# First attention of a two-layer backbone: the source's order of instructions is kept on every engine there too

## The chip, the cores and the metric

The kernel runs on one core of a Trainium2 chip. Its time is the device time of one execution in microseconds. Three runs of the kernel before took 1642.66, 1642.76 and 1645.69 us; the median is 1642.76 us. The profile was taken in an execution of its own, which took 1646.84 us.

## What is computed

The reference runs two layers over 1024 latent tokens and 256 context tokens of width 1024. Layer 0 is a windowed attention with grouped heads (16 query heads, 4 key/value heads of width 64) and a sink logit for each head; layer 1 is a latent attention. The change lies in the attention of layer 0, which for each block of 128 queries is this, cut to what matters:

```python
def attend_block(args):
    q, k, v, m = args                      # k, v: previous, own and next block of 128 keys
    s_loc = jnp.einsum("bqhgd,bkhd->bhgqk", q, k) * scale
    s_loc = jnp.where(m, s_loc, -jnp.inf)
    s_ctx = jnp.einsum("bqhgd,bchd->bhgqc", q, kc) * scale
    p = softmax_with_sink(jnp.concatenate([s_loc, s_ctx], axis=-1), sink_b)
    return (jnp.einsum("bhgqk,bkhd->bqhgd", p[..., :3 * BLOCK], v)
            + jnp.einsum("bhgqc,bchd->bqhgd", p[..., 3 * BLOCK:], vc))
...
yx = (ox * jax.nn.silu(gx)) @ w_out
```

Context queries attend to the 256 context keys alone. The result of the layer, `x + gate * yx`, goes into layer 1.

## The kernel before

**Stages.** The kernel builds normalized inputs, projects them to queries, keys, values and gates (loop over `order`, lines 772 to 797), runs the first attention with its output projection (loop over `units`, from line 816), projects for layer 1, runs the second attention and ends with the output projection of layer 1. Products are made in two or three pieces: every operand is split into a high part (a cast, ScalarE, line 121) and a remainder (a subtraction, VectorE or GpSimd, line 122), and `mm3` multiplies high by high, low by high and high by low (lines 126 to 128).

**The first attention.** There are ten tiles of 128 tokens (two of context, eight of latents), taken in the order 2, 0, 3, 1, 4, 5, 6, 7, 8, 9, and four groups of heads for each: 40 units, `UnitA`. A unit covers four heads. A latent tile inside the sequence has five chunks of 128 keys (three local, two context); tiles 2 and 9, at the ends, have four; a context tile has two. In what follows units are counted from 0 in this order, so units 0 to 3 are tile 2, units 4 to 7 context, 8 to 11 tile 3, 12 to 15 context, 16 to 35 the five inner tiles 4 to 8, 36 to 39 tile 9.

A unit goes through these steps, each with its engine:

- `score(h)`, four times: two matmuls each (591, 592) for the 256 context keys and for the local keys, two VectorE operations (598) that mask, move the scores to SBUF and keep a running minimum, and one ScalarE exponential (599). Three PSUM banks (0, 1, 2) take the scores in turn.
- `T(ci)` for each chunk: four TensorE transposes (618), a ScalarE cast (121) and a VectorE subtraction (122).
- `PV(ci)` for each chunk: two matmuls (628) that add into the one bank that `psv` has, bank 5.
- `post` and `post2`: a GpSimd subtraction (605), a small ScalarE exponential for the sink (606), a GpSimd addition (610), a VectorE reciprocal (611) and a GpSimd copy (613).
- `fin`: four ScalarE copies (638, 639 twice) that take the result out of bank 5.
- `fin2`, in the next unit: two transposes (647), a ScalarE copy (649) and five GpSimd operations (651, 652, 653, 655, 656).

The output projection of a tile is a generator (`outproj`), of which a part is taken between the steps of the next tile's units: groups of six matmuls (126 to 128), and at each half's end a VectorE product (676) and a GpSimd addition (677).

The source is software pipelined. While unit `u` does its transposes and products, it also issues scores 2 and 3 of the next unit `nu` (lines 830 to 832) and scores 0 and 1 of the one after, `nnu` (850 to 853); transposes run two chunks ahead (`next_T`). Within an inner unit with five chunks the source says, chunk by chunk: score 2 of `nu`, `fin2` of the unit before, T, PV(0), `post`; score 3 of `nu`, T, PV(1), `post2`; T, PV(2), score 0 of `nnu`; T, PV(3); T, PV(4), score 1 of `nnu`; `fin`.

**What sets the order.** The kernel is written in Tile. Tile finds the dependencies and sets the semaphores, and its scheduler orders the instructions of each engine by its own estimate of when they are ready, so that what stands in an engine's stream need not stand there in the order of the source. Inside `tc.manual_schedule()` every engine's instructions keep the order in which the source issues them. Before the change this holds from line 770 to line 801: for the first projection, and for the four scores of unit 0 that are written there. All later code, the first attention included, is ordered by the scheduler. On the chip each engine then takes its stream as it stands.

The function that holds all of this, with its line numbers, is this:

Of the kernel before, what the change touches and what calls it, by code (L numbers as in the profile page):

```python
# [33 lines left out]
class Ring:  # L34
# [6 lines left out]
    def next(self):  # L41
        b = self.bufs[self.i % len(self.bufs)]
        self.i += 1
        return b


def shp(ap, *dims):
    n = 1
    for d in dims:
        n *= d  # L50
    ap = ap[:, 0:n]
    if len(dims) == 1:
        return ap
    names = "abcdefg"[: len(dims)]
    kw = {c: d for c, d in zip(names[1:], dims[1:])}
    return ap.rearrange("p (" + " ".join(names) + ") -> p " + " ".join(names), **kw)
# [3 lines left out]
def kernel(ctx: ExitStack, tc: tile.TileContext, t, out, dbg=None):  # L60
# [63 lines left out]
    def mm3(o, a, b, first, last):  # L124
        (ah, al), (bh, bl) = a, b
        nc.tensor.matmul(o, ah, bh, start=first, stop=False)  # L126
        nc.tensor.matmul(o, al, bh, start=False, stop=False)  # L127
        nc.tensor.matmul(o, ah, bl, start=False, stop=last)  # L128
# [132 lines left out]
    def src0(i):  # L261
        if i < 2:
            return t["ctx"][i * 128 : i * 128 + 128, :]
        return t["x"][(i - 2) * 128 : (i - 1) * 128, :]
# [12 lines left out]
    def next_item():  # L277
        item[0] += 1
        todo = [x for x in due if x[0] <= item[0]]
        due[:] = [x for x in due if x[0] > item[0]]  # L280
        for _, fn in todo:
            fn()
# [375 lines left out]
    def outproj(ti, og, last=False):  # L658
        x = xr0.next()
        load(out=x, in_=src0(ti))  # L660
        gate = gx if ti >= 2 else gc
        cs = [slice(c * 512, c * 512 + 512) for c in range(2)]
        order = [(0, 0, 8), (1, 0, 8)]
        if last:
            order = [(0, 0, 6), (1, 0, 6), (0, 6, 8), (1, 6, 8)]
        ps = [None, None]
        for c, ka, kb in order:
            if ka == 0:
                ps[c] = PB[:, 0, :] if last and c else pso()
            for k in range(ka, kb):  # L670
                mm3(ps[c], [og[:, s, k, :] for s in range(2)], [Wo[k][:, s, cs[c]] for s in range(2)], k == 0, k == 7)
                if k % 2:
                    yield
            if kb == 8:
                y = ytmp.next()
                nc.vector.tensor_mul(y, ps[c], gate[:, cs[c]])
                (nc.vector if last else nc.gpsimd).tensor_add(x[:, cs[c]], x[:, cs[c]], y)
        load(out=x1_d[ti * 128 : ti * 128 + 128, :], in_=x)
# [91 lines left out]
    in_order = tc.manual_schedule()  # L770
# [27 lines left out]

    while due:
        next_item()  # L800
    in_order.__exit__(None, None, None)
    units[1].score(0)
    units[1].score(1)
    tq = iter([(u, c) for u in units for c in range(u.m)])
# [1 line left out]
    def next_T():  # L806
        n = next(tq, None)
        if n:
            n[0].T(n[1])
# [6 lines left out]
    for ui, u in enumerate(units):  # L816
        if ui in (1, 2):
            next(wo_fill, None)
            next(wo_fill, None)
        if u.g == 0:  # L820
            og = shp(ogr.next(), 2, 8, 128)
            steps = 4 * u.m - 2
            done = 0
        nu = units[ui + 1] if ui + 1 < len(units) else None
        nnu = units[ui + 2] if ui + 2 < len(units) else None
        at = {}
        for h in range(2, 4):
            at.setdefault(min(h - 2, max(0, u.m - 3)), []).append(h)
        for ci in range(u.m):
            if nu:  # L830
                for h in at.get(ci, ()):
                    nu.score(h)
            if ci == 0:
                while fins:
                    fins.pop()()
                if nnu:
                    nnu.prep()
                if ui + 3 < len(units):
                    units[ui + 3].prep_q()
            i = u.g * u.m + ci - 1  # L840
            if u.m == 2 and i > 0 and done < -(-8 * i // steps):
                next(filler, None)
                done += 1
            next_T()
            u.PV(ci)
            if ci == 0:
                u.post()
            if ci == 1:
                u.post2()
            if nnu:  # L850
                for h, at0 in enumerate((max(0, u.m - 3), u.m - 1)):
                    if ci == at0:
                        nnu.score(h)
            while i > 0 and done < -(-8 * i // steps):
                next(filler, None)
                done += 1
        u.fin(og)
        fins.append(u.fin2)
        if u.g == 3:
            for _ in filler:  # L860
                pass
            filler = outproj(u.ti, og, last=nu is None)
    units[-1].fin2(fast=True)
    last_outproj = filler

# [694 lines left out]
```

## Time and profile before

| | us |
|---|---|
| median of three runs | 1642.76 |
| the profiled execution | 1646.84 |
| its span, first to last instruction | 1645.1 |
| TensorE matmuls busy | 1587.5 (96%) |
| VectorE busy | 948.7 (58%) |
| ScalarE busy | 825.1 (50%) |
| GpSimd busy | 829.5 (50%) |
| from the end of the first projection to the last transposes (647) of the first attention | 366.92 to 731.27 in the span |

The profile names the engines PE (TensorE matmuls), PEld (its weight loads), DVE (VectorE), ACT (ScalarE), POOL (GpSimd) and SP (the queue that issues most DMAs). `L598` is line 598. A row of the timeline gives the start in us from the start of the span, how long the row lasts, the engine, the line, the operation, what is written and read, the shape, and in brackets how long the engine had been idle and what ended that. Rows of the same operation that follow one another are merged, with their count behind an x. An operation can start before the one ahead of it on its engine has quite ended, so the time from start to start is the cost of one. A unit's place in the trace is found by the pair of transposes L647: the first of them, at 378.97 us, stands in unit 1, the last, at 731.27 us, behind unit 39.

### The profile page before, as it was taken

What the parts mean: (1) busy time and instruction counts of PE and PEld (TensorE: products, weight loads), DVE (VectorE), ACT (ScalarE), POOL (GpSimd) and SP (SyncE); (2) the same over time, 40 slices, a digit from 0 to 9 for tenths busy, and PEclk for the clock granted to TensorE, in tenths of its full rate; (3) what the DMA queues carried; (4) which work ended last, traced back from release to release, by engine and by line L of the source; (5) the groups of instructions that cost most, each with busy time, mean ns of one, the idle gap of its engine ahead of it and who ended that gap; (6) DMA issues with size and microseconds to landing.
All of it is one profiled execution on the core that took longest, in us unless ns stands there. A gap on an engine that the chain in (4) does not pass through costs nothing.

```text
span 1645.1 us, 23587 instructions
## 1 busy us (share of the span) xinstructions
PE 1587.5 (96%) x8156; PEld 1214.1 (74%) x8156; DVE 948.7 (58%) x1692; ACT 825.1 (50%) x1779; POOL 829.5 (50%) x896
## 2 busy tenths in 40 slices
PE   7899999988999999998999999999999999999998
PEld 2687888776878888878887887566766756666687
DVE  1786778537757777768444005655455455455354
ACT  3622122239877778777323324555555555555421
POOL 1453356214654444444245422786676777668510
PEclk9999999989999999999999999999999999999999
DMA  8535544364333333235127722211111111122151
GB/s 280 169 115 181 170 163 167 126 197 140 94 116 95 96 91 91 90 112 173 52 78 249 233 66 87 77 52 36 39 39 36 45 37 39 46 80 70 47 160 64
DMA packets 122464, 176.74 MB, mean 107 GB/s; under 512 B 11484, under 2 KB 71516, under 8 KB 122344
## 3 DMA queue, kind: packets, MB, share of 16 engines
q1 hardware_dynamic: 120184, 171.12, 32.5%
q10 hardware_dynamic: 2160, 4.11, 0.8%
q8 instruction: 64, 1.05, 0.3%
q14 instruction: 56, 0.46, 0.1%
HBM read 129.04 MB, written 46.15 MB: 106 GB/s over the span
## 4 chain that ended last, share of the span: by engine, by line
PE 78%; DVE 6%; ACT 6%; issue 4%; POOL 3%; DMA 2%; POOLq 0%; DVEq 0%; SPq 0%; ACTq 0%
PE PB L126 17%; PE PB L128 16%; PE PB L127 16%; PE PB L1233 9%; PE PB L628 4%; PE PB L1199 4%; PE PB L618 3%; PE PB L591 2%; PE PB L592 2%; ACT arena_r L121 1%; DVE arena_r L122 1%; ACT arena_f L599 1%; DVE arena_f L202 1%; DVE arena_f L385 1%; PE PB L1258 1%
## 5 line engine op out<-in xcount | busy, mean ns | idle before, releaser
L126 PE MATMUL PB<-arena_r 128*128 128x512 f32 (+3 forms) x1632 | 607.3, 373 | 7.2 <-ACT arena_r L205 3.8
L127 PE MATMUL PB<-arena_r 128*128 128x512 f32 (+3 forms) x1632 | 597.2, 366 | 4.5 <-DVE arena_r L207 3.1
L128 PE MATMUL PB<-arena_r 128*128 128x512 f32 (+3 forms) x1632 | 594.7, 366 | 0.2 <-DVE arena_r L122 0.2
L126 PEld LDWEIGHTS PB<-arena_r 128*128 128x128 f32 (+1 forms) x1632 | 310.1, 190 | 98.3 <-issue 32.8
L1225 POOL TENSOR_TENSOR arena_f<-arena_f 128x512 f32<-128x512 f32 x252 | 327.1, 1298 | 75.2 <-ACT arena_f L1218 60.1
L128 PEld LDWEIGHTS PB<-arena_r 128*128 128x128 f32 (+1 forms) x1632 | 309.5, 190 | 49.8 <-issue 0.9
L127 PEld LDWEIGHTS PB<-arena_r 128*128 128x128 f32 (+1 forms) x1632 | 310.8, 190 | 47.0 <-DVE arena_r L207 4.5
L1218 ACT ACTIVATE arena_f<-PB 128x512 f32<-128x512 f32 x320 | 188.9, 597 | 125.2 <-PE PB L128 112.9
L1203 DVE TENSOR_REDUCE arena_f<-PB 128x1 f32<-128x1280 f32 x128 | 190.5, 1488 | 104.2 <-PE PB L1199 101.7
L122 DVE TENSOR_TENSOR arena_r<-PB,arena_r 128x512 fp32r<-128x512 f32 (+4 forms) x255 | 163.4, 647 | 138.0 <-ACT arena_r L121 136.5
L122 POOL TENSOR_TENSOR arena_r<-arena_f,arena_r 128x512 fp32r<-128x512 f32 x84 | 116.6, 1400 | 184.1 <-ACT arena_r L121 164.9
L121 ACT CAST arena_r<-PB 128x512 fp32r<-128x512 f32 (+4 forms) x255 | 139.5, 551 | 73.6 <-PE PB L618 36.9
L598 DVE CUSTOM_DVE_ANT_0 arena_f<-PB,arena_f,small 128x256 f32<-128x256 f32 (+1 forms) x288 | 145.1, 524 | 30.8 <-PE PB L592 23.0
L1233 PE MATMUL PB<-arena_f 128*64 128x512 f32 x640 | 157.1, 600 | 0.0
L599 ACT ACTIVATE arena_f<-arena_f,small 128x640 f32<-128x640 f32 (+2 forms) x160 | 119.1, 747 | 27.0 <-DVE small L598 26.6
L628 PE MATMUL PB<-arena_r 128*128 128x512 f32 x336 | 122.7, 439 | 5.6 <-ACT arena_f L639 5.3
L385 DVE SCALAR_TENSOR_TENSOR arena_f<-arena_f,small 128x512 f32<-128x512 f32 x98 | 114.1, 1209 | 11.3 <-DMA arena_f<-ada_w 11.0
L121 ACT CAST arena_r<-arena_f 128x512 fp32r<-128x512 f32 (+1 forms) x124 | 72.8, 608 | 75.0 <-DMA arena_f<-a_w_in 21.1
L618 PE MATMUL PB<-ident,arena_f 128*128 128x128 f32 x672 | 107.2, 275 | 1.2 <-ACT arena_f L649 0.6
L1233 PEld LDWEIGHTS PB<-arena_f 128*64 128x64 f32 x640 | 43.5, 136 | 80.9 <-issue 79.4
L1199 PE MATMUL PB<-arena_r 96*128 96x512 f32 (+1 forms) x384 | 99.8, 367 | 0.3 <-DVE arena_f L1203 0.2
L618 PEld LDWEIGHTS PB<-ident,arena_f 128*128 128x128 f32 x672 | 83.2, 141 | 18.2 <-ACT arena_f L599 2.3
(150 smaller groups left out, 1751.7 us busy)
## 6 DMA issues: line engine op xcount, KB each, us to landing
arena_r<-q_d SPq DMA_DIRECT2D x160, 128.0 KB, 2.9
arena_f<-ada_w SPq DMA_DIRECT2D x68, 256.0 KB, 3.0
arena_f<-a_w_in SPq DMA_DIRECT2D x40, 256.0 KB, 3.7
arena_f<-x SPq DMA_DIRECT2D x16, 512.0 KB, 4.6
q_d<-arena_f SPq DMA_DIRECT2D x16, 512.0 KB, 2.6
qn_d<-arena_f SPq DMA_DIRECT2D x16, 512.0 KB, 5.0
arena_r<-qn_d SPq DMA_DIRECT2D x32, 256.0 KB, 3.6
arena_f<-ada_w SPq DMA_DIRECT2D x14, 512.0 KB, 6.2
```

The costliest lines, as they stand in the source:

```text
L121: nc.scalar.copy(hi, src)
L122: (lo_eng or nc.vector).tensor_sub(lo, src, hi.bitcast(F32))
L126: nc.tensor.matmul(o, ah, bh, start=first, stop=False)
L127: nc.tensor.matmul(o, al, bh, start=False, stop=False)
L128: nc.tensor.matmul(o, ah, bl, start=False, stop=last)
L618: nc.tensor.transpose(pt[:, h, :], self.Ps[h][:, ci * 128 : ci * 128 + 128], ident)
L628: nc.tensor.matmul(self.pv, V[:, self.chunks[ci], self.g, :], PT[:, s], start=ci == 0 and s == 0, stop=ci == self.m - 1 and s == 1,)
L1199: nc.tensor.matmul(psm[:, n0 : n0 + n], self.qT[0:96, 0, b * 128 : b * 128 + 128], kt[0:96, 0, n0 : n0 + n], start=True, stop=True,)
L1203: nc.vector.reduce_max(self.mx[:, 96 + b : 97 + b], psm[:, 0:TOK], AX.X, negate=True)
L1218: nc.scalar.activation(E, S, AF.Exp)
L1225: eng.tensor_add(self.acc, self.acc, E)
L1233: nc.tensor.matmul(self.pv[p : p + 64], Vq[:, c, self.h % 4, :], self.E.pop(c), start=c < 2, stop=c >= NT - 2)
```

## The change

The end of the part in which the source's order is kept moves from line 801, ahead of the first attention, to a place behind the loop over its units. The last unit's `fin2` and what follows are ordered by the scheduler as before. No instruction is added, removed or altered.

```diff
     while due:
         next_item()
-    in_order.__exit__(None, None, None)
     units[1].score(0)
     units[1].score(1)
     tq = iter([(u, c) for u in units for c in range(u.m)])
...
             for _ in filler:
                 pass
             filler = outproj(u.ti, og, last=nu is None)
+    in_order.__exit__(None, None, None)
     units[-1].fin2(fast=True)
     last_outproj = filler
```

Two places show what the streams look like. The first is ScalarE's at the border between two units of an inner tile (`fin` is 638 and 639, the exponentials of the scores are 599, the cast of a transpose 121, the copy of `fin2` 649, the sink's exponential 606). Before:

```order
L121 CAST arena_r<-PB 128x512
L638 COPY arena_f<-PB 64x256
L639 COPY arena_f<-PB 64x256
L638 COPY arena_f<-PB 64x256
L639 COPY arena_f<-PB 64x256
L649 COPY arena_f<-PB 128x256
L121 CAST arena_r<-PB 128x512
L599 ACTIVATE arena_f,small<-arena_f,small 128x640 x2
L121 CAST arena_r<-PB 128x512
L599 ACTIVATE arena_f,small<-arena_f,small 128x640
L606 ACTIVATE small<-small 128x4
```

And after the change, at the same border:

```order
L599 ACTIVATE arena_f,small<-arena_f,small 128x640
L638 COPY arena_f<-PB 64x256
L639 COPY arena_f<-PB 64x256
L638 COPY arena_f<-PB 64x256
L639 COPY arena_f<-PB 64x256
L599 ACTIVATE arena_f,small<-arena_f,small 128x640
L649 COPY arena_f<-PB 128x256
L121 CAST arena_r<-PB 128x512
L606 ACTIVATE small<-small 128x4
L599 ACTIVATE arena_f,small<-arena_f,small 128x640
L121 CAST arena_r<-PB 128x512 x2
```

The exponential of `nnu`'s score 1 has moved ahead of the four copies of `fin`, that of `nu`'s score 2 ahead of 649, and 606 has moved from behind the exponential of score 3 to a place ahead of it.

The second place is TensorE's stream at the same border (591 and 592 are the score matmuls, 628 the products with V, 647 the transposes of `fin2`, 618 those of a chunk). Before:

```order
L628 MATMUL PB<-arena_r 128x512 x2
L591 MATMUL PB<-arena_r 128x256
L592 MATMUL PB<-arena_r 128x256
L591 MATMUL PB<-arena_r 128x384
L592 MATMUL PB<-arena_r 128x384
L591 MATMUL PB<-arena_r 128x256
L592 MATMUL PB<-arena_r 128x256
L647 MATMUL PB<-ident,arena_f 128x128 x2
L618 MATMUL PB<-ident,arena_f 128x128 x4
L591 MATMUL PB<-arena_r 128x384
L592 MATMUL PB<-arena_r 128x384
L628 MATMUL PB<-arena_r 128x512 x2
```

And after:

```order
L628 MATMUL PB<-arena_r 128x512 x2
L591 MATMUL PB<-arena_r 128x256
L592 MATMUL PB<-arena_r 128x256
L591 MATMUL PB<-arena_r 128x384
L592 MATMUL PB<-arena_r 128x384
L591 MATMUL PB<-arena_r 128x256
L592 MATMUL PB<-arena_r 128x256
L591 MATMUL PB<-arena_r 128x384
L592 MATMUL PB<-arena_r 128x384
L647 MATMUL PB<-ident,arena_f 128x128 x2
L618 MATMUL PB<-ident,arena_f 128x128 x4
L628 MATMUL PB<-arena_r 128x512 x2
```

The fourth pair of score matmuls has moved from behind the transposes to a place ahead of them; the rest is the same.

GpSimd's stream for a unit is alike in both: 651, 652, 653, 655, 656 of the unit before, then 605, 610 and 613 of this one.

## The prediction

> **What bounds the kernel now.** I read the page first, then the busy time of each stage of the first attention, then the timeline of one border between two units.
>
> ```profile
> span 1645.1 us, 23587 instructions
> PE 1587.5 (96%) x8156; PEld 1214.1 (74%) x8156; DVE 948.7 (58%) x1692; ACT 825.1 (50%) x1779; POOL 829.5 (50%) x896
> ```
>
> TensorE is busy 96% of the span. The stretches below run from the last matmul of the first projection to the first L647, then unit by unit as the front counts them: units 1 to 3, 4 to 7 (context), 8 to 11, 12 to 15 (context), 16 to 35, 36 to 39. Columns are length, then busy time and count of PE, PEld, DVE, ACT and POOL, then the granted clock and the DMA's share and rate.
>
> ```profile
> 366.92:378.97 12.05, 10.57 (x61) 8.45 (x60) 8.81 (x27) 10.56 (x21) 1.49 (x2) 0.86 0.52 153
> 378.97:403.28 24.31, 20.95 (x128) 16.45 (x127) 18.47 (x61) 22.30 (x61) 14.79 (x27) 1.00 0.42 125
> 403.28:429.37 26.09, 23.52 (x136) 19.33 (x137) 15.93 (x53) 22.20 (x66) 17.83 (x36) 1.00 0.32 91
> 429.37:468.31 38.94, 38.39 (x233) 33.06 (x232) 28.41 (x81) 30.74 (x77) 19.77 (x35) 1.00 0.31 96
> 468.31:496.67 28.36, 26.77 (x149) 21.42 (x147) 16.27 (x57) 20.72 (x62) 17.11 (x33) 1.00 0.43 131
> 496.67:699.51 202.84, 200.14 (x1202) 173.99 (x1201) 155.01 (x451) 161.85 (x384) 95.96 (x171) 1.00 0.31 92
> 699.51:731.27 31.76, 31.11 (x184) 26.10 (x183) 20.50 (x64) 23.26 (x59) 16.83 (x30) 1.00 0.19 65
> ```
>
> Units 16 to 35 take 202.84 / 20 = 10.14 us each, and TensorE is idle for 2.7 us of the 202.84: they are bound by TensorE, with ScalarE 80% and VectorE 76% busy beside it. So nothing is to be won there, and the question is whether the source's order still lets ScalarE, VectorE and GpSimd run ahead of TensorE. The front stages leave TensorE idle for 1.48 + 3.36 + 2.57 + 0.55 + 1.59 = 9.6 us.
>
> The border between two inner units, on TensorE (transposes of the last chunk's turn, product with V, transposes of `fin2`, next transposes, PV(0) of the new unit):
>
> ```profile
> 556.56 0.60 PE L618 MATMUL PB<-ident,arena_f 128*128 128x128 f32 x4
> 556.91 0.71 PE L628 MATMUL PB<-arena_r 128*128 128x512 f32 x2
> 557.47 0.28 PE L591 MATMUL PB<-arena_r 128*128 128x256 f32 x1
> ...
> 558.06 0.28 PE L591 MATMUL PB<-arena_r 128*128 128x256 f32 x1
> ...
> 558.31 0.38 PE L647 MATMUL PB<-ident,arena_f 128*128 128x128 f32 x2
> 558.52 0.60 PE L618 MATMUL PB<-ident,arena_f 128*128 128x128 f32 x4
> ...
> 559.47 0.68 PE L628 MATMUL PB<-arena_r 128*128 128x512 f32 x2
> ```
>
> and on ScalarE:
>
> ```profile
> 557.25 0.59 ACT L121 CAST arena_r<-PB 128x512 fp32r<-128x512 f32 x1 [0.35 <-PE PB L618]
> 557.86 0.37 ACT L638 COPY arena_f<-PB 64x256 f32<-64x256 f32 x1
> ...
> 559.00 0.37 ACT L639 COPY arena_f<-PB 64x256 f32<-64x256 f32 x1
> 559.39 0.37 ACT L649 COPY arena_f<-PB 128x256 f32<-128x256 f32 x1
> ...
> 560.13 0.84 ACT L599 ACTIVATE arena_f<-arena_f,small 128x640 f32<-128x640 f32 x1
> ...
> 560.96 0.83 ACT L599 ACTIVATE arena_f<-arena_f,small 128x640 f32<-128x640 f32 x1
> ...
> 561.77 0.58 ACT L121 CAST arena_r<-PB 128x512 fp32r<-128x512 f32 x1
> 562.25 0.83 ACT L599 ACTIVATE arena_f<-arena_f,small 128x640 f32<-128x640 f32 x1
> ...
> 563.17 0.21 ACT L606 ACTIVATE small<-small 128x4 f32<-128x4 f32 x1
> ```
>
> ScalarE empties bank 5 (638, 639) at once, until 559.37, and PV(0) of the next unit, which writes that bank, starts 0.10 us later. 606 comes last, behind three exponentials.
>
> **The change, step by step.** No instruction goes or comes; each engine takes its stream in another order. In the new order ScalarE's stream, from one 606 to the next, is: 606, exponential of score 3, casts, exponential of `nnu`'s score 0, two casts, exponential of `nnu`'s score 1, `fin`, exponential of `nu`'s score 2, 649, a cast, 606. Two waits close this into a loop. First, `fin` stands behind an exponential that waits for two VectorE operations, which wait for the subtraction of the last transposes. Second, 606 waits for 605, which stands on GpSimd behind the five operations of `fin2`, which wait for `fin` and for 649; and behind 606 on ScalarE are queued the exponential of score 3 and the casts that the next transposes and products need. The VectorE and GpSimd prices:
>
> ```profile
> 554.70 0.47 DVE L598 CUSTOM_DVE_ANT_0 arena_f<-PB,arena_f,small 128x256 f32<-128x256 f32 x1
> ...
> 555.32 0.62 DVE L598 CUSTOM_DVE_ANT_0 arena_f<-PB,arena_f,small 128x384 f32<-128x384 f32 x1
> ...
> 557.87 0.69 DVE L122 TENSOR_TENSOR arena_r<-PB,arena_r 128x512 fp32r<-128x512 f32 x1 [0.42 <-ACT arena_r L121]
> 558.48 0.47 DVE L598 CUSTOM_DVE_ANT_0 arena_f<-PB,arena_f,small 128x256 f32<-128x256 f32 x1
> ...
> 563.69 0.18 DVE L611 RECIPROCAL small<-small 128x4 f32<-128x4 f32 x1 [0.61 <-POOL small L610]
> ```
>
> ```profile
> 555.98 0.83 ACT L599 ACTIVATE arena_f<-arena_f,small 128x640 f32<-128x640 f32 x1 [0.49 <-DVE small L598]
> ```
>
> ```profile
> 560.14 0.74 POOL L652 TENSOR_TENSOR arena_f<-arena_f 128x256 f32<-128x256 f32 x1
> ...
> 562.93 0.21 POOL L605 TENSOR_TENSOR small<-small 128x4 f32<-128x4 f32 x1
> ```
>
> A score's two VectorE operations, one behind the other, and on to the exponential: (555.32 - 554.70) + (555.98 - 555.32) = 1.28. Cast to its subtraction: 557.87 - 557.25 = 0.62; subtraction to the next: 0.61. Exponential to the next: 0.82 (560.13, 560.96, 561.77). `fin`: 557.86 to 559.37, 1.51. GpSimd from 652 to 605: 2.79; 605 to 606: 562.93 to 563.17, 0.24.
>
> The loop of a full inner unit is then: 606 0.21; exponential 0.82; cast to subtraction 0.62; two subtractions 1.22; the reciprocal between them 0.18; score 0 of `nnu` 1.28; its exponential 0.82; casts and subtractions of two transposes 0.62 + 1.22; score 1 of `nnu` 1.28; its exponential 0.82; `fin` 1.51; exponential 0.82; 649 0.37; GpSimd 2.79; and 0.24. Sum 14.82 us, against 10.14 now. TensorE stays ahead of this loop: its own work in a unit is the 10.0 us of the present (200.14 / 20), and it waits mainly at PV(0), for `fin`. The loop decides, and 20 units cost 20 x 4.68 = **93.6 us** more.
>
> The other stages, by the same loop with the terms that their units have. Exponentials of shorter rows cost (mean in ns behind the bar's first number):
>
> ```profile
> L599 ACT ACTIVATE arena_f<-arena_f,small 128x512 f32<-128x512 f32 x24 | 17.4, 725 | 4.4 <-DVE small L598 4.3
> L599 ACT ACTIVATE arena_f<-arena_f,small 128x256 f32<-128x256 f32 x32 | 16.2, 508 | 1.2 <-DVE small L598 1.1
> ```
>
> - Units 1 to 3 (four chunks): one subtraction less (0.61), four exponentials of 512 (0.4 less) and two shorter VectorE operations (0.2 less): 13.6. Where `nnu`, then `nu` too, is a context unit, a second VectorE operation and longer exponentials fall away: 12.0 and 11.5. With four casts of weights (0.62 each) that stand in the stream, 39.6 against 24.31: **+15.3**.
> - Context units: 0.21 + 0.50 + 0.62 + 0.61 + 0.57 (one VectorE operation of 0.47 and the 0.10 of a hand-off, as from 559.37 to 559.47) + 0.50 + 1.51 + 1.0 + 0.37 + 2.79 + 0.24 = 8.9; 10.3 and 10.9 for the last two, which score full units. Four take 39.0, against 26.09 and 28.36: **+12.9** and **+10.6**.
> - Units 8 to 11: 14.8, 14.8, 12.7, 12.1 (the last two score context): 54.5 against 38.94, **+15.5**.
> - Units 36 to 39: 13.6 twice, then no more scores of `nnu`; 10 for unit 38 and 7 for the last, which have few or no exponentials to wait for (estimates on both sides of the present 31.76 / 4 = 7.9): 44.2 against 31.76, **+12.4**.
> - Ahead of the first L647 there is no `fin2` yet; the scores and casts of unit 1 stand in line. Between 0 and 3 us more; I take **+1.5**.
> - Behind the attention the code is scheduled as before, and its loads go into buffers that the last exponentials free: between -3 and +3, taken as **0**.
>
> SP's queue keeps the source's order too, with `prep_q` three units and `prep` two units ahead, that is over 20 us, for transfers that land within 2.9 us of their issue (the last column):
>
> ```profile
> arena_r<-q_d SPq DMA_DIRECT2D x160, 128.0 KB, 2.9
> ```
>
> I cost it at nothing. If a store of `x1_d` that waits for GpSimd held loads up, that cover would be gone; it is in the upper end. The two VectorE products of `outproj` a tile, one of which falls into the loop, are in the upper end as well (0.6 us a tile, 5 us in all).
>
> Sum: 93.6 + 15.3 + 12.9 + 10.6 + 15.5 + 12.4 + 1.5 = 161.8 us. The profiled execution took 1646.84 and would take 1808.6; it lies 4.1 us above the median, so I predict 1642.76 + 161.8 = 1804.6, **1805 us**. The own range of this case is 1775 to 1835: 0.1 us more or less at each of some ten hand-offs of the loop would be 1 us in each of 39 units, and I take three quarters of that on either side.
>
> [...]
>
> ```profile
> 353.03:356.44 3.41, 1.22 (x8) 0.84 (x7) 1.43 (x2) 2.90 (x4) 1.27 (x1) 1.00 0.71 194
> 356.44:359.85 3.41, 3.04 (x12) 2.80 (x13) 2.98 (x14) 1.97 (x5) 0.00 (x0) 0.50 0.81 224
> 359.85:363.27 3.42, 3.42 (x18) 3.42 (x17) 0.70 (x5) 1.38 (x5) 0.80 (x3) 0.50 0.98 279
> ```
>
> 2.2 us idle were followed by 6.8 us at half clock. In the new order TensorE idles about 3 us at each border, so this is to be expected there. A half-speed window takes 1.7 us of TensorE's work, and TensorE has about 4.8 us a unit to spare, so the sum stays; a pair of windows is a rival below. [...]
>
> **The rivals.**
>
> *Only the first wait binds.* If GpSimd reaches 605 early enough that 606 holds nothing, a border costs what `fin` waits: from the last transposes 557.25 - 556.56 = 0.69, then 0.62 + 0.61 + 1.28 + 0.82 + 1.51 + 0.10 = 5.63 us, against 2.65 us of TensorE's work ahead of PV(0) (0.35 + 0.56 + 0.21 + 0.35 by the starts above, and two scores of 558.06 - 557.47 = 0.59 each). 2.98 us idle at three borders of four, 1.4 less where a group of output matmuls stands between: 2.6 us on 9.9, 12.5 a unit, +48 for units 16 to 35 and at the same half of the sum +34 elsewhere: **1725 us**. For it: the present trace has 605 in the same place without harm. Against: there 606 stands behind three exponentials. 10%.
>
> *The clock binds as well.* With pairs of half-speed windows TensorE is late by some 2 us in the two units of four that have a group of output matmuls between PV(0) and the last transposes: 20 units, +40, **1845 us**. 9%.
>
> *The source's order is better.* If the loop's parts overlap by 4.7 us a unit or more, so that it is shorter than TensorE's 10.1, only the idle time of the front stages is at stake, 9.6 + 2.7 + 0.6 = 12.9 us at most: **1630 us**. For it: in the middle tiles the two orders are nearly alike. Against: it takes an exponential that doesn't wait for its scores. 3%. That it changes nothing, 2%.
>
> **How the numbers follow.** My forecast has 76%. The low end, 1740, is the own range's end and then half way to the first rival, the high end, 1850, takes in the clock's; left out are the first rival, the better order and no change, 15%, and some of the tails. Differences under 0.2% (3.3 us, about what a measurement of this kernel can tell from none) have 2%, faster 3%, slower 95%.
>
> **What would show it.** In the profile after, a pair of L647 every 14.8 us in units 16 to 35; ScalarE idle ahead of 606 with POOL L605 as what ended it, and ahead of 599 with DVE L598; TensorE idle ahead of 628 with ACT L639; PE busy about 70% of that stretch. Wrong would be: borders every 12.5 us with no idle time ahead of 606 (first rival), or TensorE without idle time at half clock (second), or every 10 us (third).

## The result, and the profile after

The changed kernel took 1867.31 us (median of four runs, 1866.13 to 1869.23) against 1643.76 us before in the same comparison: a ratio of 1.1359, 95% interval 1.1341 to 1.1377. The direction was as predicted, and so was the time of an ordinary unit; the whole lies 62 us above the forecast and above the range's end of 1850. The page of the profile after, its span and the busy time of each engine:

```profile
span 1865.6 us, 23612 instructions
PE 1671.2 (90%) x8156; PEld 1271.3 (68%) x8156; DVE 950.4 (51%) x1692; ACT 829.7 (44%) x1779; POOL 832.4 (45%) x896
```

VectorE, ScalarE and GpSimd are as long busy as before; the span has grown by 220.5 us. The stages, in the same stretches and columns as in the prediction (ahead of the first L647, units 1 to 3, 4 to 7, 8 to 11, 12 to 15, 16 to 35, 36 to 39):

```profile
366.60:387.02 20.42, 11.33 (x62) 9.59 (x61) 10.72 (x32) 11.23 (x22) 2.47 (x4) 0.88 0.29 84
387.02:430.54 43.52, 28.57 (x116) 22.65 (x115) 17.94 (x51) 22.54 (x58) 15.58 (x26) 0.66 0.18 52
430.54:473.97 43.43, 33.14 (x150) 26.29 (x149) 17.20 (x59) 23.01 (x64) 17.62 (x33) 0.84 0.25 73
473.97:535.30 61.33, 45.79 (x229) 38.32 (x228) 27.04 (x78) 30.93 (x76) 18.89 (x34) 0.86 0.20 61
535.30:578.52 43.22, 32.38 (x151) 25.85 (x149) 17.87 (x60) 23.08 (x64) 18.91 (x34) 0.88 0.29 86
578.52:904.41 325.89, 247.96 (x1202) 206.69 (x1200) 155.09 (x451) 161.22 (x380) 94.60 (x170) 0.84 0.19 58
904.41:953.80 49.39, 38.98 (x194) 30.86 (x192) 20.72 (x63) 23.83 (x61) 18.94 (x34) 0.93 0.17 56
```

Every stage of the first attention is longer, and TensorE is idle for 325.89 - 247.96 = 77.9 us in units 16 to 35 where it was idle for 2.7. Behind the last L647 the program takes 1865.6 - 953.80 = 911.8 us, against 913.8. So all of the loss is in the attention. What TensorE and ScalarE wait for in units 16 to 35 (the waits of each engine: total, times, longest):

```profile
ACT arena_f L599 <- DVE small L598: 81.3, 40, 2.4
ACT small L606 <- POOL small L605: 52.1, 20, 2.6
ACT arena_r L121 <- PE PB L618: 29.3, 9, 5.3
```

```profile
PE PB L628 <- ACT arena_f L639: 38.6, 20, 2.3
PE PB L591 <- DVE small L598: 20.1, 19, 2.5
PE PB L126 <- DVE arena_f L676: 19.3, 5, 5.1
```

The first two rows of ScalarE and the first of TensorE are the waits of the forecast loop, 20 times each for 606 and for PV(0). An ordinary unit, on ScalarE, GpSimd and TensorE, from one L647 to the next:

```profile
644.35 0.38 PE L647 MATMUL PB<-ident,arena_f 128*128 128x128 f32 x2
644.64 0.83 ACT L599 ACTIVATE arena_f<-arena_f,small 128x640 f32<-128x640 f32 x1 [2.04 <-DVE small L598]
...
647.13 1.22 PE L628 MATMUL PB<-arena_r 128*128 128x512 f32 x2 [1.96 <-ACT arena_f L639]
...
651.28 0.21 POOL L605 TENSOR_TENSOR small<-small 128x4 f32<-128x4 f32 x1
651.52 0.21 ACT L606 ACTIVATE small<-small 128x4 f32<-128x4 f32 x1 [2.61 <-POOL small L605]
...
655.60 0.83 ACT L599 ACTIVATE arena_f<-arena_f,small 128x640 f32<-128x640 f32 x1 [2.10 <-DVE small L598]
...
659.22 0.38 PE L647 MATMUL PB<-ident,arena_f 128*128 128x128 f32 x2
```

14.87 us from L647 to L647; the forecast loop was 14.82. The forecast did not name TensorE's second row either, the wait of a score's matmul for its bank; ordinary units keep 14.87 us with it. What lengthens units is the last row of each list of waits: L126 waits five times, 19.3 us in all, for VectorE's L676, and casts on ScalarE wait up to 5.3 us for transposes. The five waits of L126 and the five longest of the casts stand in the third unit of each tile (18, 22, 26, 30, 34), which takes 20 to 21 us. Unit 18, between 606 and the late cast:

```profile
615.55 0.21 ACT L606 ACTIVATE small<-small 128x4 f32<-128x4 f32 x1 [2.60 <-POOL small L605]
...
617.07 0.69 DVE L122 TENSOR_TENSOR arena_r<-PB,arena_r 128x512 fp32r<-128x512 f32 x1 [2.22 <-ACT arena_r L121]
617.67 0.17 DVE L611 RECIPROCAL small<-small 128x4 f32<-128x4 f32 x1
617.76 0.66 DVE L676 TENSOR_TENSOR arena_f<-PB,arena_f 128x512 f32<-128x512 f32 x1
...
618.47 0.80 PE L126 MATMUL PB<-arena_r 128*128 128x512 f32 x1 [3.63 <-DVE arena_f L676]
...
619.92 0.63 PE L126 MATMUL PB<-arena_r 128*128 128x512 f32 x1
...
622.35 0.59 ACT L121 CAST arena_r<-PB 128x512 fp32r<-128x512 f32 x1 [5.32 <-PE PB L618]
```

The products of the output projection have one PSUM bank. L676 empties it of a tile's first half; in the source it is issued by the generator step that also begins the second half, and in VectorE's stream it stands behind a subtraction that hangs on 606. So L126 of the second half holds TensorE for 3.63 us, and the transposes queued behind it come late to the loop.

Ahead of the first L647, the timeline shows ScalarE's cast of output weights, VectorE's subtraction of it, and the first scores of unit 1:

```profile
368.65 1.13 ACT L121 CAST arena_r<-arena_f 128x512 fp32r<-128x512 f32 x2
...
369.81 1.34 DVE L122 TENSOR_TENSOR arena_r<-arena_f,arena_r 128x512 fp32r<-128x512 f32 x1 [8.63 <-ACT arena_r L121]
371.07 0.47 DVE L598 CUSTOM_DVE_ANT_0 arena_f<-PB,arena_f,small 128x256 f32<-128x256 f32 x1
...
371.61 0.39 PE L591 MATMUL PB<-arena_r 128*128 128x256 f32 x1 [4.11 <-DVE small L598]
```

VectorE stands idle for 8.63 us at a subtraction of weights while scores wait behind it, and TensorE stops for 4.11 us. In the kernel before, VectorE was idle there for 5.40 us and took scores next, at 367.36 us.

### The profile page after: what moved, and what is told of

It reads as the page before. It is cut to its first block, busy times and chain, and to the rows that moved or that the text cites. A ratio compares the mean times of both kernels' runs of the same rounds, so it can differ in the third digit from the quotient of the medians.

```text
span 1865.6 us, 23612 instructions
## 1 busy us (share of the span) xinstructions
PE 1671.2 (90%) x8156; PEld 1271.3 (68%) x8156; DVE 950.4 (51%) x1692; ACT 829.7 (44%) x1779; POOL 832.4 (45%) x896
## 3 DMA queue, kind: packets, MB, share of 16 engines
q10 hardware_dynamic: 2160, 4.11, 0.7%
## 4 chain that ended last, share of the span: by engine, by line
PE 63%; ACT 12%; DVE 11%; POOL 6%; issue 6%; DMA 2%; SPq 0%; DVEq 0%; ACTq 0%; POOLq 0%
PE PB L126 15%; PE PB L128 14%; PE PB L127 14%; PE PB L1233 8%; ACT arena_f L599 5%; DVE arena_r L122 4%; PE PB L1199 4%; DVE arena_f L598 3%; ACT arena_r L121 2%; PE PB L628 2%; PE PB L618 2%; ACT arena_f L639 1%; POOL arena_f L652 1%; POOL arena_f L653 1%; POOL arena_r L656 1%
## 5 line engine op out<-in xcount | busy, mean ns | idle before, releaser
L126 PE MATMUL PB<-arena_r 128*128 128x512 f32 (+3 forms) x1632 | 612.0, 377 | 38.9 <-DVE arena_f L676 30.2
L126 PEld LDWEIGHTS PB<-arena_r 128*128 128x128 f32 (+1 forms) x1632 | 312.9, 192 | 134.9 <-DVE arena_f L676 34.7
L127 PEld LDWEIGHTS PB<-arena_r 128*128 128x128 f32 (+1 forms) x1632 | 314.0, 192 | 50.3 <-DVE arena_r L207 6.3
L128 PEld LDWEIGHTS PB<-arena_r 128*128 128x128 f32 (+1 forms) x1632 | 312.9, 192 | 51.9 <-issue 1.7
L628 PE MATMUL PB<-arena_r 128*128 128x512 f32 x336 | 143.5, 514 | 56.0 <-ACT arena_f L639 55.7
L121 ACT CAST arena_r<-PB 128x512 fp32r<-128x512 f32 (+4 forms) x255 | 135.2, 547 | 82.9 <-PE PB L618 47.4
L618 PE MATMUL PB<-ident,arena_f 128*128 128x128 f32 x672 | 126.6, 316 | 15.1 <-ACT arena_f L599 15.1
L591 PE MATMUL PB<-arena_r 128*128 128x256 f32 (+1 forms) x288 | 97.4, 351 | 43.9 <-DVE small L598 41.3
L618 PEld LDWEIGHTS PB<-ident,arena_f 128*128 128x128 f32 x672 | 100.5, 165 | 36.0 <-ACT arena_f L599 19.6
L651 POOL TENSOR_TENSOR arena_f<-arena_f 128x256 f32<-128x256 f32 x39 | 29.5, 756 | 211.0 <-ACT arena_f L639 211.0
L628 PEld LDWEIGHTS PB<-arena_r 128*128 128x128 f32 x336 | 63.9, 235 | 65.0 <-ACT arena_f L639 64.2
```

The source lines that it names most:

```text
L618: nc.tensor.transpose(pt[:, h, :], self.Ps[h][:, ci * 128 : ci * 128 + 128], ident)
L628: nc.tensor.matmul(self.pv, V[:, self.chunks[ci], self.g, :], PT[:, s], start=ci == 0 and s == 0, stop=ci == self.m - 1 and s == 1,)
```

## The experiments

Two theories came from this reading: the two waits of the forecast (606 behind `fin2`, `fin` behind an exponential) are the loop, and undoing both brings units back to 10 us; and L676 makes the long units. A third came after e4: in the source's order the exponentials make ScalarE and VectorE take turns. Diffs are against the changed kernel if nothing else is said. Each ratio is to the kernel before, with its 95% interval; "units 16 to 35" is that stretch's length in the profile (202.84 us before, 325.89 after).

| run | us | ratio | units 16 to 35 |
|---|---|---|---|
| e1_product_at_once | 1835.27 | 1.1156 (1.1129 to 1.1182) | 306.97 |
| e2_post_ahead_of_fin2 | 1901.26 | 1.1559 (1.1526 to 1.1593) | 345.31 |
| e3_fin_ahead_of_score | 1824.14 | 1.1090 (1.1062 to 1.1118) | 302.31 |
| e4_all_three | 1801.67 | 1.0950 (1.0921 to 1.0979) | 287.55 |
| e5_exp_behind_casts | 1746.06 | 1.0609 (1.0592 to 1.0626) | 248.51 |
| e6_sink_exp_a_chunk_later | 1717.49 | 1.0439 (1.0424 to 1.0455) | 237.69 |
| e7_and_product_at_once | 1677.67 | 1.0191 (1.0174 to 1.0208) | 211.08 |
| e8_weights_later | 1866.64 | 1.1344 (1.1327 to 1.1361) | 325.42 |
| e10_score_behind_transposes | 1698.28 | 1.0330 (1.0313 to 1.0347) | 223.38 |
| e11_that_source_scheduled | 1645.31 | 1.0010 (1.0000 to 1.0019) | 203.61 |
| e12_in_order_from_unit_16 | 1782.25 | 1.0844 (1.0828 to 1.0861) | 322.88 |
| e13_and_weights_later | 1700.08 | 1.0342 (1.0324 to 1.0359) | 222.03 |

**e1: the product of a half right behind its matmuls.**

```diff
-                if k % 2:
+                if k % 2 and k < 7:
                     yield
...
                 (nc.vector if last else nc.gpsimd).tensor_add(x[:, cs[c]], x[:, cs[c]], y)
+                yield
```

> The changed kernel, with the VectorE product of the output projection (L676) and its addition issued right behind the half's last matmuls instead of one generator step later; nothing else differs. Theory A: one unit of each tile is long (18 to 21 us instead of 14.9 in the inner tiles) since the first matmul of the second half waits for the bank that L676 frees, and L676 stands on VectorE behind a subtraction and the reciprocal L611, which wait for GpSimd by way of 606. Then the long units go (all near 14.9, no idle time ahead of L126 that L676 ends), and their excess, 45 us over nine units, comes back: about 1822 us. Theory B: the long units are long because the TensorE clock halves at the borders; then they stay at 18 us or more and the time at 1855 to 1867 us.

32 us less, where Theory A had 45. No matmul waits for L676 any more, and the long units shrink (unit 18: 15.89 us instead of 21.08, unit 22: 15.75). In units 16 to 35 ScalarE's wait for transposes is down from 29.3 us:

```profile
ACT arena_r L121 <- PE PB L618: 4.4, 5, 1.1
```

But units 17, 18 and 19 take 15.47, 15.89 and 15.52 us, together some 2 us a tile above 14.88. In 17 and 19 one of the two products stands in VectorE's part of the loop. Unit 18 has none; there output matmuls run at half clock (0.50 granted from 604.70 to 608.10 us), and a cast still waits 1.09 us for the transposes behind them, so, as an estimate from that wait, some 1 us of a long unit goes with the clock. The rest does not. In e1's unit 18 the same matmuls run at the same 0.63 us, but without a wait ahead of them:

```profile
606.28 0.63 PE L126 MATMUL PB<-arena_r 128*128 128x512 f32 x1
...
607.56 0.63 PE L126 MATMUL PB<-arena_r 128*128 128x512 f32 x1
```

**e2: `post` and `post2` at the unit's start**, ahead of score 2 of `nu` and of `fin2`.

```diff
+        u.post()
+        u.post2()
         for ci in range(u.m):
...
-            if ci == 0:
-                u.post()
-            if ci == 1:
-                u.post2()
```

> The changed kernel, with post and post2 of a unit (605, 606, 610, 611, 613) issued ahead of fin2 of the unit before; nothing else differs. Theory A, the loop of the prediction: the GpSimd leg of 2.79 us leaves the loop, and what remains is fin behind an exponential; a full unit takes 12.5 to 12.9 us instead of 14.9, ScalarE no longer idles ahead of 606, the long units shrink too since the reciprocal is early, about 1760 us. Theory B, the first rival of the prediction turned round: GpSimd's leg does not bind, only the order of fin and the exponential does; then the units stay at 14.9 and the time within 10 us of 1867.

Slower, by 34 us, which neither theory had. 606 waits for nothing now, but the reciprocal 611 stands ahead of score 2's operations on VectorE and waits for it:

```profile
678.18 0.18 DVE L611 RECIPROCAL small<-small 128x4 f32<-128x4 f32 x1 [3.01 <-POOL small L610]
...
679.54 0.83 ACT L599 ACTIVATE arena_f<-arena_f,small 128x640 f32<-128x640 f32 x1 [1.68 <-DVE small L598]
```

The wait for 606 has moved to VectorE (57.2 us in units 16 to 35), where it holds an exponential that had not waited there.

**e3: `fin` ahead of score 1 of `nnu`.**

```diff
+            if ci == u.m - 1:
+                u.fin(og)
             if nnu:
...
-        u.fin(og)
```

> The changed kernel, with fin issued ahead of score 1 of nnu in the last chunk; nothing else differs. Theory A, the loop of the prediction: fin's 1.5 us leave the loop, the GpSimd leg stays; a full unit takes about 13.3 us, the long units stay long, about 1815 us. Theory B, only the wait of fin binds: a full unit takes about 10.2 us, about 1690 us.

43 us less; most full units take 13.6 or 14.2 us. The long units stay, and the wait for L676 in them is now the dearest of TensorE's in units 16 to 35:

```profile
PE PB L126 <- DVE arena_f L676: 30.0, 5, 6.0
```

**e4: the edits of e1, e2 and e3 together.**

> The changed kernel with the edits of the three runs before together. Theory A: no loop is longer than TensorE's own work in a unit; a full unit takes 10.2 to 10.6 us, and what is left over the kernel before is mostly the start, where TensorE waits 4.1 us behind the split of the output weights: 1645 to 1680 us. Theory B, the in-order streams or the halved clock cost something beside the three places: full units above 11.5 us, above 1700 us.

ScalarE no longer waits ahead of 606, nor TensorE for `fin` or L676, and yet most units take 14.2 to 14.9 us. The first theory falls, though a piece of the first loop is left: as in e2, the reciprocal 611 waits on VectorE for 610, and that for 606:

```profile
DVE small L611 <- POOL small L610: 27.3, 20, 1.4
```

That is 1.4 us a unit; an estimate from these numbers is that without it a unit would take some 12.9 us, still far from 10. ScalarE and VectorE, in half a unit:

```profile
629.81 0.83 ACT L599 ACTIVATE arena_f<-arena_f,small 128x640 f32<-128x640 f32 x1 [1.68 <-DVE small L598]
...
631.03 0.59 ACT L121 CAST arena_r<-PB 128x512 fp32r<-128x512 f32 x1
631.65 0.69 DVE L122 TENSOR_TENSOR arena_r<-PB,arena_r 128x512 fp32r<-128x512 f32 x1 [1.87 <-ACT arena_r L121]
...
632.89 0.62 DVE L598 CUSTOM_DVE_ANT_0 arena_f<-PB,arena_f,small 128x384 f32<-128x384 f32 x1
633.55 0.83 ACT L599 ACTIVATE arena_f<-arena_f,small 128x640 f32<-128x640 f32 x1 [1.93 <-DVE small L598]
634.37 1.05 ACT L121 CAST arena_r<-PB 128x512 fp32r<-128x512 f32 x2
```

They take turns. An exponential waits for its score's VectorE operations; the casts of transposes that are long done are queued behind the exponential; their subtractions stand on VectorE ahead of the next score, whose exponential waits again. ScalarE waits so 80 times in units 16 to 35, at each of their four exponentials, 125.9 us in all. This second loop lies beside the first; with the 1.4 us at 611 in it, it is nearly as long.

**e5: an exponential goes behind the casts of the next transposes.** `score` only notes its exponential, and `next_T` issues it behind its own cast, unless those transposes need it. The source edits of e2 and e3 are not in it.

```diff
+            if UnitA.held is None:
+                ex()
+            else:
+                UnitA.held.append((self, ex))
...
+    def let_go():
+        while UnitA.held:
+            UnitA.held.pop(0)[1]()
...
     def next_T():
         n = next(tq, None)
         if n:
+            if any(v is n[0] for v, _ in UnitA.held or ()):
+                let_go()
             n[0].T(n[1])
+        let_go()
...
+    UnitA.held = []
```

> The changed kernel, with every exponential of a score in the attention loop issued behind the casts of the next chunk's transposes instead of right behind its score; the streams of the other engines stay as they are. Theory A, turns: in the source's order ScalarE and VectorE work in turns, since each exponential stands ahead of casts whose subtractions stand ahead of the next score's VectorE operations, and a unit takes nearly the sum of both engines' work (8.0 + 7.5 us). With casts first both run side by side: a full unit takes 10.5 to 11.5 us, still with some idle time ahead of 606, about 1705 us. Theory B, the loop of the prediction by way of GpSimd and 606 is what holds a unit: then little is gained, full units at 13.5 us or more, above 1800 us.

121 us less than the change, the largest step of all, and this one edit undoes more than e4's three, though the time stays 41 us above what Theory A had. It does not touch the second loop alone: the exponential of `nnu`'s score 1 is now held past `fin`, as e3 had it (at one border `fin` starts at 597.04 us and that exponential at 599.98), and TensorE no longer waits for `fin`. So the 121 us are the second loop and one of the two forecast waits together; e3 alone brought 43. ScalarE's waits ahead of exponentials fall from 81.3 us to 13.4; of the forecast wait at 606 and of L676 there is left in that stretch:

```profile
ACT small L613 <- POOL small L612: 26.6, 20, 2.9
ACT arena_f L601 <- DVE small L599: 13.4, 12, 1.4
```

```profile
PE PB L126 <- DVE arena_f L683: 16.1, 5, 3.2
```

(In e5, e6, e7, e10, e11 and e13 lines have moved: 599 is 601, 598 is 599, 591 is 592, 605 and 606 are 612 and 613, 618 is 625, 676 is 683.)

**e6: e5, and `post` and `post2` a chunk later.**

```diff
-            if ci == 0:
-                u.post()
             if ci == 1:
+                u.post()
+            if ci == min(2, u.m - 1):
                 u.post2()
```

> The run before (exponentials behind the casts), with post issued in chunk 1 and post2 in chunk 2 instead of 0 and 1. Theory A: what is left of the wait for GpSimd ahead of 606 goes, a full unit takes 10.1 to 10.4 us, one unit a tile stays some us longer since L676 waits on VectorE: about 1680 us. Theory B, the wait for GpSimd is nothing once the exponentials have moved: the same time as the run before.

**e7: e6 with the edit of e1.**

> The run before, with the product L676 issued right behind the half's last matmuls too. Theory A: all full units at 10.1 to 10.4 us, about 1660 us, and what is left over the kernel before is at the start. Theory B, L676 was only late because everything was: no difference to the run before.

28.6 us less, and 39.8 less again; both end above what was expected. In e7 the units 16 to 35 take 10.55 us each, and ScalarE's stream at the border has the order listed for the kernel before: a cast, `fin`, the copy of `fin2`, a cast, two exponentials, a cast, an exponential, the sink's. Of the 32 us that its median is above before, the context units 4 to 7 and 12 to 15 make most: 35.92 and 36.01 us against 26.09 and 28.36; units 16 to 35 make 8.2. In the full units TensorE waits for a third score bank (the stretch 500 to 712 us):

```profile
PE PB L592 <- DVE small L599: 10.5, 15, 1.7
```

**e10: e7, with score 2 of `nu` behind the transposes**. In the kernel before, the scheduler has only the second pair of its matmuls there.

```diff
-            if nu:
+            if nu and (u.m == 2 or ci):
...
             next_T()
+            if nu and u.m > 2 and ci == 0:
+                nu.score(2)
```

> In e7 TensorE still waits 14.5 us, in 20 waits of up to 1.7 us, at a unit's border for VectorE to empty the third score bank, since score 1 of the unit after next and score 2 of the next stand there one behind the other (four pairs of matmuls, three banks); here score 2 of a full unit goes behind the fin2 transposes and the next chunk's transposes. Theory A (that bank is what remains in the full units): units 16 to 35 go from 211.1 to 202 to 205 us and the whole from 1677.7 to 1664 to 1670. Theory B (VectorE is behind as a whole, so the wait moves to PV or to the next transposes): 1674 or more.

21 us slower than e7, so Theory A falls. The subtraction of those transposes now stands on VectorE ahead of score 2's operations and waits for its cast, so the bank comes free late all the same:

```profile
572.45 0.69 DVE L122 TENSOR_TENSOR arena_r<-PB,arena_r 128x512 fp32r<-128x512 f32 x1 [0.55 <-ACT arena_r L121]
...
573.59 0.44 PE L592 MATMUL PB<-arena_r 128*128 128x384 f32 x1 [1.03 <-DVE small L599]
```

That is not all of it: in units 16 to 35 TensorE's wait for the bank grows only from 10.2 to 14.9 us, and the stretch by 12.3. The edit moves one thing more. Exponentials are held until the next casts, so that of score 2 goes a chunk later too (at this border behind a cast that waits until 575.18 us), and ScalarE's wait for transposes grows from 31.5 to 53.7 us. Which of the two makes e10 slower was not separated.

**e8 and e13: the last two pieces of output weights one unit later**, in the changed kernel and in e10.

```diff
-        if bi >= 8 and gp != 1:
+        if bi >= 8 and gp != 1 and (bi, gp) != (9, 0):
...
-        if ui in (1, 2):
+        if ui in (1, 2, 3):
```

> The changed kernel, with the last two pieces of output weights split one unit later, so that their subtraction does not stand on VectorE ahead of unit 1's first scores; nothing else differs. Theory A: TensorE's wait of 4.1 us at the end of the first projection goes, and some of the half clock behind it: 3 to 8 us less than the changed kernel. Theory B, another wait takes its place (the exponentials of unit 0 behind the table load): less than 2 us.

> e10 and the last two pieces of output weights one unit later, as in e8. In e8 ScalarE was the bound in unit 3 and the 3.2 us won ahead of the first L647 went back there. Theory A (with the exponentials moved, unit 3 has room for the casts): 2 to 5 us under e10. Theory B (the casts cost there as much as ahead): within 1 us of e10.

The time is the same in both. In e8 the first L647 comes at 383.81 instead of 387.02, and unit 3, where the casts go, takes 15.21 instead of 12.24. In e13 it is 379.74 instead of 382.01, and units 1 to 3 take 32.75 instead of 29.83. What is won ahead is given back.

**e11: the source of e10, scheduled as before the change.**

> The source of e10, with the exit from the source's order where it stood before the change, so the first attention is scheduled again. Theory A (the scheduler finds the same order from either source; the source's order costs only where it is taken literally): 1640 to 1650. Theory B (the scheduler follows the source among what is ready, so that this source does better or worse under it too): under 1637 or over 1653.

1645.31 against 1643.92: no difference that counts. From a source that costs 54 us when taken literally, the scheduler makes the same time as from the old one.

**e12: the source's order from unit 16 on alone.**

```diff
+    in_order.__exit__(None, None, None)
     units[1].score(0)
...
+        if ui == 16:
+            in_order = tc.manual_schedule()
+            in_order.__enter__()
```

> The changed kernel, with the source's order only from unit 16 on; units 0 to 15 are scheduled as before. Theory A (each unit is late by its own loop, and the stages add up): 1643.8 + (325.9 - 202.8) + (49.4 - 31.8) - 2 = 1782, between 1774 and 1790. Theory B (what the earlier stages leave behind, the clock or a late transfer, makes part of the later units' loss): under 1770.

1782.25 us, where Theory A had 1782. The stretches are units 1 to 15, 16 to 35 and 36 to 39:

```profile
377.13:495.46 118.33, 110.22 (x642) 90.62 (x641) 80.06 (x250) 97.25 (x265) 70.13 (x127) 1.00 0.36 105
495.46:818.34 322.88, 241.72 (x1201) 197.97 (x1200) 154.79 (x451) 160.48 (x379) 93.12 (x169) 0.89 0.19 58
818.34:867.67 49.33, 39.82 (x194) 31.43 (x192) 20.73 (x63) 23.82 (x61) 18.86 (x34) 0.90 0.18 57
```

Units 16 to 35 take 3 us less than in the changed kernel, where the units ahead of them are in the source's order too; so each unit is late by its own loop, and stages add up. No version beat the kernel before.

## Why the prediction was wrong

**The loop of a full unit was right.** 14.82 us forecast, 14.87 to 14.89 measured in ten of the twenty inner units, with the waits at 606, 599 and 628 where the prediction put them. In the unit shown above no leg of the sum is off by more than 0.15 us, so this is not luck. The first and the third rival fell: borders did not come every 12.5 us, nor every 10. The half clock was there (0.84 granted on the mean in units 16 to 35), but ordinary units kept 14.87 us through it, since the loop lies on other engines; the 1 us estimated for e1's unit 18 is what shows of the second rival. (The low end of the range is 1740 in the prediction, but half way from 1775 to the first rival's 1725 is 1750; nothing hangs on it.)

**The step that failed is the term for L676, "0.6 us a tile, 5 us in all".** It was priced as VectorE time and left to the upper end of the range; in the sum it counts nothing. What it costs is that the only bank of the output products waits for it, that TensorE's stream waits for the bank, and that the next transposes are queued behind. By the boundaries L647, the third units of the tiles took:

| unit | forecast | measured |
|---|---|---|
| 6 and 14 (context) | 10.3 each | 14.07, 14.06 |
| 10 | 12.7 | 18.62 |
| 18, 22, 26, 30, 34 | 14.82 each | 21.08, 20.69, 20.46, 19.99, 19.52 |
| 38 | 10 | 14.46 |

That is 3.8 + 3.8 + 5.9 + 27.6 + 4.5 = 45.6 us of the 58.7 by which the span missed its sum (1865.6 against 1645.1 + 161.8). e1 shows L676 as the cause of most of it: without the wait these nine units are 35.8 us shorter, 1.8 us in each context unit and 3.4 to 5.2 in the others. Some of that is lost again in other units: the stage of units 8 to 11 is shorter by 5.9 us, 16 to 35 by 18.9, 36 to 39 by 3.4, but the two context stages by only 0.1 and 0.2, since units 4, 7, 12 and 15 take 0.4 to 1.5 us longer in e1. Why they do was not settled. The step was in reach: VectorE's new stream has L676 behind a subtraction that hangs on 606, and in the source one generator step holds both the product and the matmuls that need its bank.

**Ahead of the first L647**, "between 0 and 3 us" was 20.42 - 12.05 = 8.4. The scores were costed as standing in line; that VectorE would idle for 8.63 us at a subtraction of weights ahead of them was not. e8 shows that the casts are 3.2 us of it. In e5 the first L647 comes at 382.10 instead of 387.02, so 4.9 us go with the place of the exponentials.

**The other terms** came out nearer. Without the third units, units 4 to 39 are 0.5 to 1.8 us a stage above the forecast. Units 1 to 3 took 43.52 against 39.6, where the mean clock was 0.66; what makes these 3.9 us stays open. Behind the attention the change was -2.0 against 0.

**The loop was right as a sum, but was not the whole cause.** The prediction says that two waits close the loop. e4 takes both from where they stood, and 14.2 to 14.9 us are left, since a second loop of nearly the same length lies beside it: exponential, casts, subtractions, next score, next exponential. In e4 1.4 us of that are still the wait for 606, now at 611. e5 breaks the second loop and frees `fin`, and it gives the most of any edit; how its 121 us divide between the two was not separated. What the scheduler's order does is to let ScalarE take casts that are ready, and `fin`, ahead of an exponential that is not. e5 to e7 show that for the full units, where that order on ScalarE, with the edit of e1, brings 10.55 us; what makes the last 32 us of e7 is argued from the waits alone.

## What to carry to other kernels

Where engines take their streams in order, an operation costs not its duration but all that is queued behind it on its engine while it waits, and all that waits for that on the others: follow every operation that frees a single buffer, however short (here 0.66 us of L676 cost 5.2 us in unit 18, by e1). When a loop has been found and priced, look for a second one beside it before promising what removing a wait will bring; e2 and e10 each moved an operation out of the way of a wait and were slower. A software-pipelined source that does well under a scheduler is not an order to be taken literally: here it cost 13.6%, and three hand edits (those of e7) brought back all but 1.9%.

## What the runs showed of the hardware

TensorE's granted clock fell from 1.00 to 0.50 after a stretch whose longest wait was 2.54 us. Three stretches of the changed kernel:

```profile
641.63:645.04 3.41, 1.15 (x8) 1.00 (x8) 2.75 (x7) 1.37 (x4) 0.00 (x0) 1.00 0.00 0
645.04:648.45 3.41, 1.45 (x6) 1.13 (x5) 1.20 (x5) 3.31 (x10) 1.99 (x2) 0.50 0.47 166
648.45:651.87 3.42, 3.42 (x15) 3.02 (x15) 1.72 (x5) 0.81 (x3) 2.83 (x6) 0.50 0.35 110
```

In the first TensorE was busy for 1.15 us of 3.41, and its longest wait was the one of 2.54 us ahead of an L591; the next two ran at 0.50, as after the row at 353.03 in the prediction, where it was busy for 1.22 us of 3.41. A row of 3.41 us at 0.50 is what the prediction calls a half-speed window. Whether the longest wait or the busy time of a stretch goes with the fall of the clock, these rows do not show.
